# SyncE in written order in the q/k stage: weight tiles asked for a tile ahead, four forget pages per step between them

## The chip, the cores and the metric

The kernel runs on one core of a Trainium2 chip. A core has TensorE (PE, matrix products), VectorE (DVE), ScalarE (ACT), GpSimd (POOL) and SyncE (SP), which only issues transfers; each of them works through a queue of its own in order, and they wait for each other by semaphores. The metric is the device time of one run of the whole kernel in microseconds, the median of several runs.

## The reference

One inference step of a decoder of two layers over 1024 prompt tokens, 16 meta tokens and 64 sample tokens. The change sits in the first layer's mixer, and touches what prepares the second layer's cache:

```python
def mlstm_mixer(xn, C0, n0, m0, lead, w_in, b_ig, b_fg, mh_g, w_out):
    p = xn @ w_in
    q = heads(p[..., :HK], DK_A) * DK_A ** -0.5
    k = heads(p[..., HK:2 * HK], DK_A)
    v = heads(p[..., 2 * HK:2 * HK + HV], DV_A)
    ...
    li = softcap(gi.astype(f32) + b_ig.astype(f32)).transpose(0, 2, 1)
    lf = jax.nn.log_sigmoid(softcap(gf.astype(f32) + b_fg.astype(f32))).transpose(0, 2, 1)
    h, state = mlstm_sequence(q, k, v, li, lf, state0, lead)
    ...
    out = (h.reshape(B, T, HV).astype(xn.dtype) * jax.nn.sigmoid(og)) @ w_out

def attend_sample(q, k, v, lf):
    ...
    lp = cache_logf[page_table].reshape(Bd, n_pages * PAGE_SIZE, H_B)
    c = jnp.cumsum(jnp.concatenate([lp.astype(f32), lf], axis=1), axis=1)
```

`cache_logf[page_table]` gathers, for 8 sequences, 4 pages each of log-forget values: 32 pages, whose numbers stand in a table in memory.

## The kernel before

`phase_a` is the first mixer. First `values_a` computes the values, the gates and the first pieces of what follows. Then comes the q/k stage, 126.7 to 239.7 us on TensorE: the function `qk_out` makes q and k in 8 weight tiles of 128 output channels (m = 0 to 7), each against three token groups of 336, 384 and 384 columns (`TG`). So there are 24 steps; step x works on tile x // 3 and group x % 3. Each product in f32 is built from three matmuls of halves: the input is kept as xh and xl, and a weight tile is split into whi (a cast on ScalarE) and wlo (a subtraction on VectorE, raw minus whi). A step gathers its 24 matmuls (L193 to L195) in one of two PSUM buffers (`mmA`), ScalarE evacuates it into one of three buffers `stg` (L918), and GpSimd sends it to memory (L919). Step x therefore can't begin before step x - 2 has been evacuated.

The weights are loaded by `load_w`: a buffer `wraw` (there are two), a transfer of 512 KB asked for by SyncE (L256), the cast (L259) and the subtraction (L260) into one of three pairs of buffers. Below, "w_in m" is the weight tile m of the q/k stage, and "w_out m" is piece m of the output projection's weight, which is loaded, split and sent to memory (`wo_keep`, L875) for later use; the first three pieces and w_in 0 (`self.q0`) are done in `values_a`, by `wo_fetch` (transfer, L854) and `wo_split` (L271, L272).

Between the steps other work is written, by generators that are advanced at certain steps:

- `rec_prep`, at steps 1, 4 and 9: nine transposes each of the input gates (li) and the forget gates (lf) into buffers `rps`, of which there are two, by groups of three (L1098), each group copied by ScalarE (L1100); then scans and sums of these rows on VectorE (L1106 to L1132), with three exponentials on ScalarE (L1124, L1127, L1134); at step 9 their transposes back (L1140 to L1145).
- `cache_loads`: the page table into SBUF, then for each page a read of its number from SBUF into a register of SyncE (L1008, TENSOR_LOAD with two small instructions) and the transfer of the page at that number (L1010, FUSED_REGOPS, MOVE and the request), four pages per advance, at steps 0 to 7.
- `cache_prep`, at step 14: transposes the pages, sums them up and writes them out (eight requests of GpSimd, L1027).

The order of each engine's queue is set by a scheduler from the dependences, except for engines named in `manual_schedule`, which keep the written order. In this stage only TensorE is named there. For the others the scheduler chooses: it has set the page table and its 32 reads before 48 us, far ahead of their place in the text, and the 32 page requests into one block.

Of the kernel before, what the change touches and what calls it, by code (L numbers as in the profile page):

```python
# [17 lines left out]
P = 128  # L18
# [604 lines left out]
def _add(cls):  # L623
    def deco(f):
        setattr(cls, f.__name__, f)
        return f

    return deco
# [250 lines left out]
@_add(Net)  # L879
def phase_a(self, vt):  # L880
    nc, I, O = self.nc, self.I, self.O
    w_in = I["w_in_a"][0]
    qkD = self.dram.tile([8, P, T], F32, name="qkD")
    ogD = self.dram.tile([8, P, T], F32, name="ogD")
    v = lambda i: vt[:, i * HA * (DV + 1) : (i + 1) * HA * (DV + 1)].rearrange("p (h d) -> p h d", h=HA)
    with ExitStack() as c3:
        kp = c3.enter_context(self.pool("kA"))
        tm = kp.tile([P, NT, 104], F32, name="tmA")
        den = kp.tile([P, NT, HA], F32, name="den")
        ssq = kp.tile([P, NT, HA], F32, name="ssqA")  # L890
        self.C = [kp.tile([P, 4, DV + 1], F32, name=f"C{a}") for a in range(3)]
        gates = kp.tile([P, NT, 16], F32, name="gates")
        self.fin = (tm, den, ssq)
        for i in range(NT):
            nc.gpsimd.memset(v(i)[:, :, DV : DV + 1], 1.0)
        nc.gpsimd.memset(gates, 0.0)
        nc.gpsimd.memset(tm[:, 0, :], 0.0)
        nc.gpsimd.memset(den, 1.0)
        nc.gpsimd.memset(ssq, 1.0)
        st = c3.enter_context(self.pool("stA", bufs=3))  # L900
        self.woD, self.held = [], []
        self.values_a(v, kp, gates, w_in, c3)
        pp = c3.enter_context(self.pool("ppA", bufs=2, space=PSUM))

        def wo_out():
            m = len(self.woD)
            self.wo_keep(*self.load_w([I["w_out_a"][0][:, m * P : (m + 1) * P]]))

        def qk_out():

            for m in range(8):
                wh, wl = self.load_w([w_in[:, m * P : (m + 1) * P]]) if m else self.q0
                for t, (t0, t1) in enumerate(TG):
                    n = t1 - t0
                    ps = pp.tile([P, 512], F32, name=self.uid("mmA"), tag="mmA")
                    self.fm_cols(ps[:, :n], wh, wl, self.XG[t])
                    s = st.tile([P, GL], F32, name=self.uid("stg"), tag="stg")
                    nc.scalar.activation(s[:, :n], ps[:, :n], AF.Copy, scale=DK ** -0.5 if m < 4 else 1.0)  # L918
                    nc.gpsimd.dma_start(qkD[m, :, t0:t1], s[:, :n])  # L919
                    yield  # L920

        with self.pool("rowsA") as rp, self.pool("rowsAp", bufs=2, space=PSUM) as rpp, \
                self.pool("cp") as cp, self.tc.manual_schedule(engines={mybir.EngineType.PE}):
            pages = self.cache_loads(cp)
            prep = self.rec_prep(kp, gates, rp, rpp)
            next(prep)
            for x, _ in enumerate(qk_out()):
                if x in (1, 4, 9):
                    next(prep, None)
                next(pages, None)  # L930
                if x == 14:
                    self.cache_prep(*self.cache, rpp, "r")
                if x % 3 == 0 and 5 < x < 21:
                    wo_out()

        def gates_out():

            get = lambda m, later=None: self.load_w([w_in[:, (16 + m) * P : (17 + m) * P]], later=later)
            ws = [get(0)]
            later = []  # L940
            for m in range(8):
                wh, wl = ws[m]
                for t, (t0, t1) in enumerate(TG):
                    n = t1 - t0
                    ps = pp.tile([P, 512], F32, name=self.uid("mmA"), tag="mmA")
                    xh, xl = self.XG[t]
                    if t == 1 and m < 7:
                        ws.append(get(m + 1, later if m else None))
                    for k in range(KT):
                        if k == 6 and later:  # L950
                            later.pop()()
                        self.mm3(ps[:, :n], wh[:, k, :], wl[:, k, :], xh[:, k, :], xl[:, k, :], k == 0, k == KT - 1)
                        if k == KT - 1:
                            s = st.tile([P, GL], F32, name=self.uid("stg"), tag="stg")
                            nc.scalar.activation(s[:, :n], ps[:, :n], AF.Sigmoid)
                            nc.gpsimd.dma_start(ogD[m, :, t0:t1], s[:, :n])
                        yield

        left = {t: list(range(HA)) for t in range(3)}
        left[-1] = [None]  # L960

        def heads(pp, tag, op=None, some=None):

            ready, used = [], []
            todo = [(t, h) for t in (0, 1, 2) for h in left[t]][:some]

            def ahead():
                if todo:
                    t, h = todo.pop(0)
                    og = op(self.uid("ogc")) if callable(op) else op.pop(0)  # L970
                    nc.gpsimd.dma_start(og[:, : TG[t][1] - TG[t][0]], ogD[h, :, TG[t][0] : TG[t][1]])
                    ready.append(og)

            def gate(t):
                if not left[t]:
                    return False
                while todo and (len(ready) < 3 if callable(op) else op):
                    ahead()
                if t < 0:
                    return False  # L980
                og = ready.pop(0)
                self.gate_head(t, left[t].pop(0), v, og, pp, tag)
                if not callable(op):

                    used.append(og)
                    if len(used) > 1:
                        op.append(used.pop(0))
                return True
            return gate

        self.recurrence(kp, self.rec, v, qkD, gates_out(),
                        lambda places: heads(pp, "mmA", places, 10))
    return heads
# [2046 lines left out]
```

## Time and profile before

| | |
|---|---|
| time, median of 3 runs | 2832.24 us (2831.84 to 2833.01) |
| profiled execution | 2829.72 us, its span 2828.0 us, granted clock 0.994 |
| q/k stage | 126.7 to 239.7 us, TensorE busy for 105.73 of 113.00 us, clock 0.95 |
| before it, 0 to 126.7 us | TensorE busy for 115.77 us |
| after it, 239.7 to 2828 us | TensorE busy for 2540.44 of 2588.30 us |

In the time lines a row gives the start and the duration in us, the engine ("SPq" is a request by SyncE), the line, the operation, the destination and the sources by the names of the program, the shape, how many instructions were gathered in the row, and in square brackets how long the engine stood idle before it and what ended that. A row of the windows view gives a stretch, its length, the busy time of TensorE, its weight loads, VectorE, ScalarE and GpSimd, and then the granted clock of TensorE, the share of the transfer engines and GB/s. The matmuls overlap, so a matmul of 0.34 us is followed by the next after 0.17 us.

### The profile page before, as it was taken

The page shows a single profiled execution, that of the slowest core. Times are in us where ns is not written, and L with a number is a line of the kernel's source. Part 1 is how long each engine was busy: PE and PEld are TensorE (multiplying, and loading weights), DVE is VectorE, ACT ScalarE, POOL GpSimd, SP SyncE. Part 2 cuts the span into 40 slices and gives each one's busy share as a digit, 9 for nine tenths or more (in the row PEclk, how much of TensorE's full clock was granted, in tenths as well). Part 3 has the DMA queues.
Part 4 walks back from the last instruction along what each step waited for, and adds up shares of the span by engine and source line. Part 5 has one row for each costly group of instructions (what it writes and reads, how often), then busy time and mean ns, then how long its engine had stood idle before and what let it go on. Part 6 is the DMA issues. An engine that isn't in the chain of part 4 may idle for free. (4 is left out here: it accounts for less than half of the span.)

```text
span 2828.0 us, 60538 instructions
## 1 busy us (share of the span) xinstructions
PE 2761.9 (98%) x23543; PEld 2650.3 (94%) x23543; DVE 1800.4 (64%) x4025; ACT 1177.3 (42%) x2299; POOL 836.0 (30%) x1313
## 2 busy tenths in 40 slices
PE   8999999999999999999999999999999999999998
PEld 8989889999999999999999888677999999999998
DVE  4632566888887765563455444777388888766556
ACT  5422453432322334443444445777343223323345
POOL 3122233132232332124453202544313223323111
PEclk9999999999999999999999999999999999999999
DMA  6666547245554375545444676442524555527556
GB/s 196 171 196 162 144 125 255 90 143 165 176 167 148 112 243 174 195 145 171 139 172 132 237 279 226 154 143 86 157 83 128 175 176 164 161 90 239 178 191 215
DMA packets 439001, 474.03 MB, mean 168 GB/s; under 512 B 41422, under 2 KB 365258, under 8 KB 437690
## 3 DMA queue, kind: packets, MB, share of 16 engines
q1 hardware_dynamic: 387522, 320.78, 36.8%
q0 software_dynamic: 43808, 143.17, 15.3%
q10 hardware_dynamic: 7384, 6.22, 0.7%
q8 instruction: 185, 3.03, 0.5%
q14 instruction: 102, 0.84, 0.1%
HBM read 322.84 MB, written 147.21 MB: 166 GB/s over the span
## 5 line engine op out<-in xcount | busy, mean ns | idle before, releaser
L1611 PE MATMUL m<-xh,slot 128*128 128x276 f32 x2752 | 541.3, 290 | 1.8 <-ACT fs L1640 1.8
L1611 PEld LDWEIGHTS m<-xh,slot 128*128 128x128 f32 x2752 | 440.4, 188 | 3.6 <-ACT fs L1640 2.2
L1611 PE MATMUL m<-xl,slot 128*128 128x276 f32 x1376 | 397.4, 289 | 0.0
L1611 PEld LDWEIGHTS m<-xl,slot 128*128 128x128 f32 x1376 | 259.1, 188 | 0.0
L193 PE MATMUL tmps<-slot,xh 128*128 128x256 f32 (+2 forms) x864 | 243.1, 281 | 0.0
L195 PE MATMUL tmps<-slot,xl 128*128 128x256 f32 (+2 forms) x864 | 240.6, 278 | 0.0
L194 PE MATMUL tmps<-slot,xh 128*128 128x256 f32 (+2 forms) x864 | 240.5, 278 | 0.0
L272 DVE TENSOR_TENSOR slot<-slot,slot 128x1024 fp32r<-128x1024 f32 x124 | 162.9, 1314 | 60.7 <-ACT slot L271 59.2
L271 ACT CAST slot<-slot 128x1024 fp32r<-128x1024 f32 x124 | 129.6, 1046 | 141.2 <-PE m L1611 111.7
L194 PEld LDWEIGHTS tmps<-slot,xh 128*128 128x128 f32 (+1 forms) x864 | 159.2, 184 | 0.1
L195 PEld LDWEIGHTS tmps<-slot,xl 128*128 128x128 f32 (+1 forms) x864 | 158.6, 184 | 0.0
L193 PEld LDWEIGHTS tmps<-slot,xh 128*128 128x128 f32 (+1 forms) x864 | 158.4, 183 | 0.2
L193 PE MATMUL mmA<-xh,whi 128*128 128x384 f32 (+1 forms) x384 | 135.1, 352 | 0.0
L194 PE MATMUL mmA<-xl,whi 128*128 128x384 f32 (+1 forms) x384 | 127.9, 333 | 0.0
L195 PE MATMUL mmA<-xh,wlo 128*128 128x384 f32 (+1 forms) x384 | 127.7, 333 | 0.0
L272 DVE TENSOR_TENSOR slot<-vA,slot 128x1024 fp32r<-128x1024 f32 (+1 forms) x59 | 82.2, 1396 | 32.6 <-ACT slot L271 31.5
L272 DVE TENSOR_TENSOR slot<-Ht,slot 128x1024 fp32r<-128x1024 f32 (+1 forms) x59 | 81.4, 1382 | 32.3 <-ACT slot L271 31.1
L271 ACT CAST slot<-Ht 128x1024 fp32r<-128x1024 f32 (+1 forms) x59 | 61.0, 1037 | 96.8 <-PE m L1611 92.9
L271 ACT CAST slot<-vA 128x1024 fp32r<-128x1024 f32 (+1 forms) x59 | 60.8, 1035 | 95.5 <-PE m L1611 90.5
L1715 DVE TENSOR_TENSOR ws<-ws 128x128 f32<-128x128 f32 x264 | 93.8, 355 | 8.9
L2862 ACT ACTIVATE s<-s,nb 128x272 f32<-128x272 f32 (+7 forms) x126 | 98.9, 786 | 0.0
L2897 ACT COPY th<-tp 128x768 f32<-128x768 f32 (+1 forms) x80 | 73.6, 920 | 53.7 <-PE tp L2889 30.5
(805 smaller groups left out, 8668.8 us busy)
## 6 DMA issues: line engine op xcount, KB each, us to landing
ws<-in_w_down SPq DMA_DIRECT2D x176, 128.0 KB, 2.8
sD<-ws SPq DMA_DIRECT2D x176, 128.0 KB, 2.3
slot<-sD SPq DMA_DIRECT2D x40, 512.0 KB, 4.2
slot<-in_w_gate_up SPq DMA_DIRECT2D x36, 512.0 KB, 3.9
kp<-in_cache_k SPq DMA_DIRECT2D x32, 512.0 KB, 6.7
vp<-in_cache_v SPq DMA_DIRECT2D x32, 512.0 KB, 5.1
vA<-in_w_gate_up SPq DMA_DIRECT2D x26, 512.0 KB, 4.4
Ht<-in_w_gate_up SPq DMA_DIRECT2D x26, 512.0 KB, 3.9
```

The lines of the kernel that those rows point to most:

```text
L193: mm(ps, sh, mh, start=first, stop=False)
L194: mm(ps, sh, ml, start=False, stop=False)
L195: mm(ps, sl, mh, start=False, stop=last)
L271: self.nc.scalar.copy(hi, src)
L272: self.nc.vector.tensor_tensor(out=lo, in0=src, in1=hi.bitcast(F32), op=ALU.subtract)
L1611: nc.tensor.matmul(u.ps[h, b], w[p][:, k], x[q][:, k], start=first and k == i == 0, stop=k == 3 and i == 2, skip_group_check=True)
L1715: tt(out=o, in0=a, in1=b, op=ALU.subtract)
L2862: nc.scalar.activation(ss[z, u], ss[z, u], AF.Exp, bias=nb[:, z : z + 1], accum_out=sm[:, u, z : z + 1])
L2897: nc.scalar.copy(th.rearrange("p x z (u h q) -> p h (x z u) q", h=2, q=64)[:, :, :n], pt[:, :, :n])
```

## The change

SyncE keeps the written order in the q/k stage as well. The weights of this stage are no longer loaded by `load_w` at their tile, but in two halves: `wo_fetch` asks for w_in m + 1 at the first group of tile m, and for w_out m + 2 at the second group of tiles 1 to 5; `wo_split` casts and subtracts after the second and the third group's evacuation is written. The page table, the page reads and the page requests now stand between them in the written order, four pages per step from step 1 to step 8, and `cache_prep` comes at step 13. Line numbers behind the edit rise by one or two.

```diff
         def qk_out():
 
             for m in range(8):
-                wh, wl = self.load_w([w_in[:, m * P : (m + 1) * P]]) if m else self.q0
+                wh, wl = self.q0
                 for t, (t0, t1) in enumerate(TG):
+                    if t == 0 and m < 7:
+                        self.wo_fetch(w_in[:, (m + 1) * P : (m + 2) * P])
+                    elif t == 1 and 0 < m < 6:
+                        self.wo_fetch(m + 2)
                     n = t1 - t0
...
                     nc.gpsimd.dma_start(qkD[m, :, t0:t1], s[:, :n])
+                    if self.held and t:
+                        self.wo_split()
                     yield
 
         with self.pool("rowsA") as rp, self.pool("rowsAp", bufs=2, space=PSUM) as rpp, \
-                self.pool("cp") as cp, self.tc.manual_schedule(engines={mybir.EngineType.PE}):
+                self.pool("cp") as cp, self.tc.manual_schedule(engines={E.PE, E.SP}):
...
-                next(pages, None)
-                if x == 14:
+                if x:
+                    next(pages, None)
+                if x == 13:
                     self.cache_prep(*self.cache, rpp, "r")
-                if x % 3 == 0 and 5 < x < 21:
-                    wo_out()
```

`wo_out`, the function that loaded a piece of w_out by `load_w`, is removed. `wo_split` gives the halves of a w_in tile to the next tile's steps by `self.q0`, and those of a w_out piece to `wo_keep`. `cache_loads`, `cache_prep` and `rec_prep` are unchanged.

The order on SyncE at the head of the q/k stage, before. `wraw_108`, `wraw_120` and `wraw_132` are w_in 1, 2 and 3, `wraw_125` is w_out 3, and `cp0` receives the pages; the marks leave out pages.

```order
L256 DMA wraw_108_2097<-in_w_in_a 128x8x128
L256 DMA wraw_120_2355<-in_w_in_a 128x8x128
L256 DMA wraw_125_2429<-in_w_out_a 128x8x128
L1010 ISA
L1010 DMA cp0_1904<-in_cache_logf 128x16
...
L256 DMA wraw_132_2534<-in_w_in_a 128x8x128
L256 DMA wraw_140_2594<-in_w_out_a 128x8x128
L256 DMA wraw_147_2659<-in_w_in_a 128x8x128
```

All 32 pages stand in one block between w_out 3 and w_in 3, and the reads of the table are not here. The same engine and place now; `wraw_99`, `wraw_111` and `wraw_126` are w_in 1, 2 and 3, `wraw_114` and `wraw_129` are w_out 3 and 4, and `ptab` is the table.

```order
L854 DMA wraw_99_1874<-in_w_in_a 128x8x128
L1003 DMA ptab_70<-in_page_table 1x32
L1010 TENSOR_LOAD ptab_70
L1010 ISA x2
L1012 ISA
L1012 DMA cp0_1953<-in_cache_logf 128x16
...
L854 DMA wraw_111_2063<-in_w_in_a 128x8x128
...
L854 DMA wraw_114_2133<-in_w_out_a 128x8x128
...
L854 DMA wraw_126_2330<-in_w_in_a 128x8x128
...
L854 DMA wraw_129_2400<-in_w_out_a 128x8x128
```

The table and every read of it have come into the stage; 8 pages stand ahead of w_in 2, 4 ahead of w_out 3, 8 ahead of w_in 3, 4 ahead of w_out 4 and the last 8 behind it.

On ScalarE around steps 2 to 8, before: `whi` from `wraw_125` is the cast of w_out 3, that from `wraw_132` of w_in 3, `stg_107` to `stg_119` are the evacuations of steps 2, 3, 4 and 5.

```order
L259 CAST whi_126_2430<-wraw_125_2429 128x1024
L918 ACTIVATE stg_107_2054<-mmA_106_2029 128x384
L918 ACTIVATE stg_112_2128<-mmA_111_2103 128x336
L259 CAST whi_133_2535<-wraw_132_2534 128x1024
L918 ACTIVATE stg_114_2196<-mmA_113_2171 128x384
L1100 COPY lf_1871<-rps_115_2199 8x336
L1100 COPY lf_1871<-rps_116_2204 8x384
L1100 COPY lf_1871<-rps_117_2209 8x384
L1127 ACTIVATE stk_2231<-mA_1873 8x1104
L259 CAST whi_141_2595<-wraw_140_2594 128x1024
L918 ACTIVATE stg_119_2312<-mmA_118_2287 128x384
```

The cast of w_in 3 stands ahead of step 4's evacuation and of the copies of the forget rows. The same engine and place now; `stg_110`, `stg_113`, `stg_116`, `stg_123` and `stg_128` are the evacuations of steps 2 to 6, and the copies of `lf` from `rps_120` and `rps_121` are left out.

```order
L271 CAST whi_117_2163<-wraw_111_2063 128x1024
L919 ACTIVATE stg_110_2020<-mmA_109_1995 128x384
L271 CAST whi_124_2283<-wraw_114_2133 128x1024
L919 ACTIVATE stg_113_2090<-mmA_112_2065 128x336
L919 ACTIVATE stg_116_2160<-mmA_115_2135 128x384
L1102 COPY lf_1871<-rps_119_2167 8x336
...
L271 CAST whi_132_2430<-wraw_126_2330 128x1024
L1129 ACTIVATE stk_2199<-mA_1873 8x1104
L919 ACTIVATE stg_123_2280<-mmA_122_2255 128x384
L271 CAST whi_136_2502<-wraw_129_2400 128x1024
L1126 ACTIVATE wA_1869<-wA_1869 8x1104
L1136 ACTIVATE stk_2199<-bA_1872 8x1104
L919 ACTIVATE stg_128_2357<-mmA_127_2332 128x336
```

The casts of w_in 2 and w_out 3 now stand ahead of step 2's and step 3's evacuations, the cast of w_in 3 has moved behind the copies of `lf`, and two casts stand ahead of the evacuations of steps 5 and 6.

More of the change, by code (lines that the diff above doesn't have):

```diff
@@ L881, in phase_a @@
     nc, I, O = self.nc, self.I, self.O
+    E = mybir.EngineType
     w_in = I["w_in_a"][0]
@@ L903, in phase_a @@
         pp = c3.enter_context(self.pool("ppA", bufs=2, space=PSUM))
-        def wo_out():
-            m = len(self.woD)
-            self.wo_keep(*self.load_w([I["w_out_a"][0][:, m * P : (m + 1) * P]]))
         def qk_out():
             for m in range(8):
-                wh, wl = self.load_w([w_in[:, m * P : (m + 1) * P]]) if m else self.q0
+                wh, wl = self.q0
                 for t, (t0, t1) in enumerate(TG):
+                    if t == 0 and m < 7:
+                        self.wo_fetch(w_in[:, (m + 1) * P : (m + 2) * P])
+                    elif t == 1 and 0 < m < 6:
+                        self.wo_fetch(m + 2)
                     n = t1 - t0
```

## Prediction

> **What bounds the kernel now.** I read the page first, then the list of TensorE's waits, then the time lines of TensorE, ScalarE, VectorE and SyncE over the q/k stage, from 127 to 240 us. The page:
> ```profile
> span 2828.0 us, 60538 instructions
> PE 2761.9 (98%) x23543; PEld 2650.3 (94%) x23543; DVE 1800.4 (64%) x4025; ACT 1177.3 (42%) x2299; POOL 836.0 (30%) x1313
> ```
> TensorE is busy for 98% of the span, and the change alters none of its work; what can move are TensorE's waits in this stage and the speed at which it is clocked. Its largest wait there, in the list of waits (sum, count, mean, us), and its time line around it (start, duration):
> ```profile
> PE rps L1098 <- ACT lf L1100: 6.8, 1, 6.8
> ...
> 140.11 0.32 PE L193 MATMUL mmA<-xh,whi 128*128 128x336 f32 x1
> ...
> 143.80 0.34 PE L193 MATMUL mmA<-xh,whi 128*128 128x384 f32 x1
> ...
> 147.96 0.78 PE L1098 MATMUL rps<-ident,lf_tm 80*8 80x80 f32 x6
> 155.55 0.80 PE L1098 MATMUL rps<-ident,lf_tm 128*8 128x128 f32 x3 [6.80 <-ACT lf L1100]
> 156.00 0.67 PE L193 MATMUL mmA<-xh,whi 128*128 128x384 f32 x1
> ...
> 158.39 0.48 PE L194 MATMUL mmA<-xl,whi 128*128 128x384 f32 x1
> 158.70 0.34 PE L195 MATMUL mmA<-xh,wlo 128*128 128x384 f32 x1
> ```
> Step 3 begins at 140.11, step 4 at 143.80 and ends at 147.96: a step of 336 columns takes 3.69 us, one of 384 takes 4.16. Then six transposes of forget gates run, the last three find no free PSUM buffer for 6.80 us, and step 5, begun at 156.00, runs slow until 158.6 (0.48 to 0.67 us a matmul instead of 0.34). ScalarE at that place:
> ```profile
> 144.05 0.45 ACT L918 ACTIVATE stg<-mmA 128x336 f32<-128x336 f32 x1 [2.42 <-issue]
> 153.75 1.04 ACT L259 CAST whi<-wraw 128x1024 fp32r<-128x1024 f32 x1 [9.25 <-DMA wraw<-in_w_in_a]
> 154.70 0.48 ACT L918 ACTIVATE stg<-mmA 128x384 f32<-128x384 f32 x1
> 155.08 0.78 ACT L1100 COPY lf<-rps 8x336 f32<-8x336 f32 x2
> ```
> The cast of the weight tile (w_in 3) waits 9.25 us for its transfer, and behind it stand step 4's evacuation and the copies of the forget rows (L1100), which would free the buffer. SyncE says why the tile is late:
> ```profile
> 122.86 2.64 SPq L256 DMA_DIRECT2D wraw<-in_w_in_a  x2
> ...
> 130.71 0.37 SPq L256 DMA_DIRECT2D wraw<-in_w_out_a  x1
> 131.34 18.28 SPq L1010 DMA_DIRECT2D cp<-in_cache_logf  x32
> 149.74 0.39 SPq L256 DMA_DIRECT2D wraw<-in_w_in_a  x1
> ```
> The 32 forget pages stand in one block, 18.28 us long, ahead of w_in 3, asked at 149.74. The granted clock (the third number from the end) in stretches of 10 us:
> ```profile
> 150.00:160.00 10.00, 4.45 (x19) 4.29 (x20) 5.18 (x11) 2.58 (x5) 1.18 (x2) 0.66 0.67 179
> ...
> 180.00:190.00 10.00, 10.00 (x50) 9.92 (x50) 1.51 (x3) 1.54 (x2) 0.55 (x1) 0.83 0.71 207
> ```
> At 0.66 over 4.45 busy us the slow stretch costs 4.45 x 0.34 = 1.5 us. So the place costs 6.80 + 1.5 = 8.3 us, and that is all the change can win. The second dip (10 x 0.17 = 1.7 us) follows small transposes (L1140 to L1145) that both kernels have, and I leave it in both.
>
> **The change part by part.**
>
> *The page loop.* SyncE now reads a table entry into a register and asks for its page in one go, 32 times within the stage. Before, the 32 reads (L1008) were over by 48 us. Both halves, as min/median/max ns, the one wait for the table, and the median time from asking a weight tile to its landing:
> ```profile
> L1008 SPq TENSOR_LOAD <-ptab x32: 262/275/1086, 12.7 to 47.3; - x32
> L1008 SPq FUSED_REGOPS  x32: 147/147/181, 13.2 to 47.6; - x32
> L1008 SPq SEQ_ASSERT  x32: 18/18/33, 13.4 to 47.8; - x32
> ...
> L1010 SPq FUSED_REGOPS  x32: 37/37/48, 131.1 to 149.2; - x32
> L1010 SPq MOVE cp<-in_cache_logf x32: 29/29/38, 131.3 to 149.2; - x32
> L1010 SPq DMA_DIRECT2D cp<-in_cache_logf x32: 332/333/1267, 131.3 to 149.3; - x32
> ...
> SPq L1008 <- DMA ptab<-in_page_table: 4.2, 1, 4.2
> ...
> wraw<-in_w_in_a SPq DMA_DIRECT2D x22, 512.0 KB, 4.2
> ```
> One page before took 18.28 / 32 = 0.57 us, of which 37 + 29 + 333 ns are instructions, so 0.17 is three gaps of 0.06. The read adds 0.275 + 0.147 + 0.018 + three such gaps = 0.61. **A page: 0.57 + 0.61 = 1.18 us.** Bounds: 1.07 (with every gap of the read left out, 0.57 + 0.44 = 1.01, and shortest read) up to 0.57 + 0.61 + 0.81 = 1.99, if each read were like the slowest, 1.086. I take the median, as the forget pages run at 157 to 207 GB/s or so and the slow reads fell in the first 48 us, where a stretch reached 392 GB/s:
> ```profile
> 25.00:30.00 5.00, 4.13 (x37) 3.97 (x36) 4.36 (x10) 4.05 (x10) 0.86 (x1) 1.00 1.03 392
> ...
> 140.00:150.00 10.00, 8.74 (x56) 8.29 (x54) 1.38 (x2) 1.89 (x3) 2.17 (x4) 1.00 0.53 157
> ```
> A sentence apart: the Trainium skill, "Runtime: NRT & Kernel Launch", section "Instruction fetch mechanics", gives about 200 ns for a register read; the estimate by it would be 1.10 us a page and about 1.7 us less than my sum, and the 262 ns minimum here does not agree.
>
> *Requests in written order.* Now the order is w_in 1, the table, 8 pages, w_in 2, 4 pages, w_out 3, 8 pages, w_in 3, 4 pages, w_out 4, 8 pages, then weights alone. w_in 1 is asked at 122.86 as before, so the table at 123.3 and, with the same 4.2 us of wait, the first read at 127.8. Each weight costs 0.4 to ask and 4.2 to land:
> w_in 2 asked 127.8 + 8 x 1.18 = 137.2, lands 141.4; w_out 3 asked 142.4, lands 146.6; w_in 3 asked 152.2, lands 156.4; w_out 4 asked 157.3, lands 161.5. All pages are asked by 167. The matmuls need w_in 2 at step 6 and w_in 3 at step 9, so these are early enough for TensorE itself; what bites is that ScalarE takes its queue in order, and the casts of these four now stand among evacuations.
>
> *ScalarE's queue, step by step* (cast 1.05, evacuation 0.45 to 0.48):
> Step 4 needs step 2's buffer. Cast of w_in 2 ends 142.5, evacuation of step 2 143.0, step 4 due 143.80: covered, with 0.8 to spare.
> Step 5: the cast of w_out 3 ends 147.6, then evacuations of steps 3 and 4 until 148.55 and the first forget copy until 148.95. TensorE comes to its third transposes at 147.96 + 0.78 = 148.7: a wait of 0.25 instead of 6.80. Step 5 starts at 148.95 + 0.5 = 149.45 (before: 156.00).
> Step 7 needs step 5's buffer, due 149.45 + 4.16 + 3.69 = 157.3. Ahead of that evacuation stand the cast of w_in 3 (to 157.45) and the exponential of mA (1.13, to 158.6); it ends at 159.1. **New wait 1.9 us**.
> Step 8 needs step 6's buffer, due 159.2 + 4.16 = 163.4. Ahead stand the cast of w_out 4 (161.5 to 162.6) and the exponentials of wA and bA; their rows before, and the work on VectorE that feeds them:
> ```profile
> 165.42 1.21 DVE L1122 TENSOR_TENSOR wA<-eA,mA 8x1024 f32<-8x1024 f32 x1
> ...
> 166.82 1.20 DVE L1132 TENSOR_TENSOR bA<-stk,eA 8x1024 f32<-8x1024 f32 x1
> ...
> 161.75 1.13 ACT L1127 ACTIVATE stk<-mA 8x1104 f32<-8x1104 f32 x1 [4.90 <-DVE mA L1110]
> ...
> 166.66 1.13 ACT L1124 ACTIVATE wA<-wA 8x1104 f32<-8x1104 f32 x1 [0.79 <-DVE wA L1122]
> ...
> 170.66 1.12 ACT L1134 ACTIVATE stk<-bA 8x1104 f32<-8x1104 f32 x1
> ```
> 162.6 + 1.13 + 1.12 + 0.48 = 165.3. **New wait 2.0 us**. This one has a floor: bA was ready 12.94 us after the first forget copy (166.82 + 1.20 - 155.08), so at 148.55 + 12.94 = 161.5 at best; then 1.12 and 0.48 give 163.1, against 157.3 + 4.16 = 161.5, so 1.65 remain however fast SyncE is.
> Later weights stand behind no pages: w_in 4 is asked near 167 and cast by 173, step 12 comes after 180.
>
> *Parts at nothing.* The reads leave the first 48 us; TensorE's wait there that is nearest to them, 1.99 us (row below), was for a cast, and I credit nothing; bounds nil to -2.0. Preparing the forget rows a step earlier has the same four transposes and eight requests on GpSimd (count, then busy us and mean ns):
> ```profile
> L1027 POOL DMA_DIRECT2D csE<-cp x8 | 4.3, 544 | 1.7 <-DVE clast L1025 1.3 <-issue 0.4
> ```
> GpSimd's other work there is one request a step, so evacuated tiles leave at most 4.3 us later; the three evacuation buffers, about 12 us of steps, hide that, and without them it would cost up to 4.3. Splits of weights move but keep their number.
>
> *The clock.* Does a wait of 2 us halve it? The nearest row is an early wait:
> ```profile
> 32.36 0.52 PE L193 MATMUL tmps<-whi,xh 128*80 128x272 f32 x1 [1.99 <-ACT whi L271]
> ...
> 30.00:35.00 5.00, 3.01 (x13) 2.44 (x12) 3.99 (x10) 4.02 (x12) 0.85 (x1) 0.74 0.74 199
> ```
> After 1.99 us without work the clock was 0.74 over these 5 us, so yes, once. The dip of 180 to 190 cost 1.7 in all, which I take as the price. With two waits of this size, bounds are none and 3.4 us; I take one, 1.7.
>
> **The sum.** Before 8.3; after 0.25 + 1.9 + 2.0 + 1.7 = 5.85, so -2.4 us. On the profiled execution (2829.72 us, span 2828.0) that gives 2827.3; this execution was 2.52 below the median of 2832.24, and I forecast the median: **2829.8 us**. 24 pages stand ahead of w_out 4, so 0.1 us more a page costs 2.4 us; the gain is gone at 1.18 + 2.4 / 24 = 1.28 us a page.
>
> A measurement of this kernel tells about 0.2% from no change, 5.7 us: faster is below 2826.6, slower above 2837.9.
>
> **The rivals.**
> B, *the two new waits don't touch the clock*: -2.4 - 1.7 = -4.1, 2828.1 us. For it: an overlap of a 2 us wait with busy time on both sides; against it, the row at 32.36. The Trainium skill, "TensorE: Matmul & The Clock Gate", section "What's actually happening", has the clock halved only after an idle window of about 3.4 us; by that rule B holds, while the 1.99 us wait of this trace, followed by 0.74, does not agree with it.
> C, *faster beyond doubt*: the reads run near 1.07 a page, w_out 4 lands 2.6 us sooner, step 7's wait goes and step 8's falls to its floor; with no dip 0.25 + 1.65 = 1.9 remain, so -6.4, 2825.8 us. For it: 262 to 275 ns are both minimum and median of the reads. Against it: it needs the clock to hold too.
> D, *slower: SyncE's page loop sets the pace.* Every weight now waits behind reads that SyncE can't run ahead of. If reads stretch as they did up to 1086 ns, or gaps do, each cast comes late, ScalarE holds evacuations behind it and TensorE waits at steps 4, 5, 7 and 8. From 1.18 + 8.1 / 24 = 1.52 us a page it is slower than can be missed; at 1.6 it gives -2.4 + 0.42 x 24 = +7.7, 2839.9 us, and at 1.99 some +17. For it: the maximum is four times the median, and pages have traffic beside them; against it: the median lies by the minimum.
> That SyncE's order stays as it was is excluded: the rows of the order shown with the change have the weights among the pages.
>
> **How the numbers follow.** My forecast has 0.38, B 0.20, C 0.17, D 0.25. Within 0.2% lie the forecast and B: 0.58. The range reaches to C's -6.4 with a little under it, 2825.5, and to D at 1.6 us a page, 2840; left out are slower pages than that.
>
> **What would show it.** In the profile after: the wait of the third transposes under 0.5 us; pages as triplets of a read, a register step and a request, 1.1 to 1.3 us apart from 127.8 on; casts of w_in 3 and w_out 4 released by their transfers at about 156.4 and 161.5; waits of 1 to 2.5 us ahead of steps 7 and 8 by ScalarE's evacuations; the clock under 1 once after one of them. I am wrong if pages come 1.5 us apart, if a wait over 4 us stands at step 4 or 5 (then w_in 2 or w_out 3 was later than worked out), or if the time moves outside this stage.

## The result, and the profile after

Over 20 runs each, the changed kernel takes 2834.07 us (median) and the kernel before 2831.02. The ratio on record is 1.0018 (95% interval 1.0012 to 1.0024); it isn't the quotient of these two medians, which is 1.0011. So the changed kernel is slower by some 3 to 5 us; the forecast was 2.4 us faster. The profiled execution has a span of 2829.8 us, 1.8 above that of before, so it shows less of the loss than the medians. The two lists of waits answer each other; this is TensorE's list after, from 120 to 250 us:

```profile
PE mmA L193 <- ACT stg L919: 9.8, 1, 9.8
PE rps L1100 <- ACT lf L1102: 0.7, 1, 0.7
```

The wait of 6.8 us for the forget rows has shrunk to 0.7, as meant. A single wait of 9.8 us has come in its place, for an evacuation. The first gate transposes and the first evacuation behind the stage bound it, in the time lines of TensorE and ScalarE, first before, then after:

```profile
134.57 0.78 PE L1098 MATMUL rps<-ident,gates 80*8 80x80 f32 x6
244.73 0.45 ACT L955 ACTIVATE stg<-mmA 128x336 f32<-128x336 f32 x1
```
```profile
133.21 0.78 PE L1100 MATMUL rps<-ident,gates 80*8 80x80 f32 x6
248.48 0.45 ACT L957 ACTIVATE stg<-mmA 128x336 f32<-128x336 f32 x1
```

110.16 us became 115.27, so the stage lost 5.1. Waits account for 9.8 + 0.7 - 6.8 = 3.7 of it, most of the rest is the clock, below. Around the stage this execution got some back. It began the stage 1.4 us earlier, since it had no half-speed stretch at 32 us (a second trace of the changed kernel has it again, at 33.1 us). Behind the stage it got back 1.9 us, 1.5 of them where before ran at half speed from 257.7 us on and this one didn't.

SyncE after (start, duration, count):

```profile
127.97 8.72 SPq L1012 DMA_DIRECT2D cp<-in_cache_logf  x8
136.79 0.39 SPq L854 DMA_DIRECT2D wraw<-in_w_in_a  x1
137.97 3.70 SPq L1012 DMA_DIRECT2D cp<-in_cache_logf  x4
141.77 0.39 SPq L854 DMA_DIRECT2D wraw<-in_w_out_a  x1
142.96 9.56 SPq L1012 DMA_DIRECT2D cp<-in_cache_logf  x8
152.62 0.39 SPq L854 DMA_DIRECT2D wraw<-in_w_in_a  x1
154.13 3.71 SPq L1012 DMA_DIRECT2D cp<-in_cache_logf  x4
159.67 0.39 SPq L854 DMA_DIRECT2D wraw<-in_w_out_a  x1
160.85 9.90 SPq L1012 DMA_DIRECT2D cp<-in_cache_logf  x8
170.85 0.47 SPq L854 DMA_DIRECT2D wraw<-in_w_in_a  x1
```

The weights are asked for almost at the forecast times: w_in 2 at 136.8 (137.2), w_out 3 at 141.8 (142.4), w_in 3 at 152.6 (152.2). Then ScalarE and TensorE:

```profile
163.53 1.04 ACT L271 CAST whi<-wraw 128x1024 fp32r<-128x1024 f32 x1 [14.40 <-DMA wraw<-in_w_in_a]
164.60 1.12 ACT L1129 ACTIVATE stk<-mA 8x1104 f32<-8x1104 f32 x1
165.74 0.49 ACT L919 ACTIVATE stg<-mmA 128x384 f32<-128x384 f32 x1
```
```profile
166.29 0.69 PE L193 MATMUL mmA<-xh,whi 128*128 128x384 f32 x1 [9.82 <-ACT stg L919]
```

The cast of w_in 3 begins 10.9 us after its transfer was asked for, not 4.2; behind it stand the exponential and step 5's evacuation, and step 7 waits for that. So it is the path that the prediction gave for step 7, with a far longer landing. The transfers issued from 148 to 160 us (KB, median us to landing), and the windows view around them (transfer share and GB/s at the end of a row):

```profile
woD<-wlo POOLq DMA_DIRECT2D x1, 512.0 KB, 10.8
wraw<-in_w_in_a SPq DMA_DIRECT2D x1, 512.0 KB, 10.8
...
out_s_m<-mA POOLq DMA_DIRECT2D x1, 0.2 KB, 9.9
out_p_m<-mA POOLq DMA_DIRECT2D x1, 0.0 KB, 9.5
```
```profile
150.00:152.00 2.00, 2.00 (x14) 2.00 (x13) 2.00 (x2) 0.00 (x0) 0.64 (x1) 1.00 1.02 368
152.00:154.00 2.00, 2.00 (x14) 2.00 (x13) 2.00 (x2) 0.00 (x0) 0.00 (x0) 1.00 0.38 81
154.00:156.00 2.00, 2.00 (x15) 2.00 (x14) 2.00 (x2) 0.00 (x0) 0.52 (x1) 1.00 1.57 57
156.00:158.00 2.00, 0.47 (x4) 0.19 (x2) 0.40 (x1) 0.00 (x0) 0.00 (x0) 1.00 0.77 28
158.00:160.00 2.00, 0.00 (x0) 0.00 (x0) 0.00 (x0) 0.00 (x0) 0.00 (x0) 1.00 0.40 17
```

The transfer engines are occupied, yet move 17 to 81 GB/s: single packets of w_in 3 take up to 5.9 us, against 27 ns for the median packet of its size. Two very small writes are in flight, both outputs of the layer asked by GpSimd: out_s_m, 64 numbers of 4 bytes each for scattered places (at 150.05), and out_p_m, 8 numbers (at 154.28). Before, out_s_m was asked at 157.74, and from 160 to 164 us nothing else was on the way:

```profile
160.00:162.00 2.00, 2.00 (x14) 2.00 (x13) 2.00 (x2) 0.24 (x1) 0.00 (x0) 1.00 0.00 0
162.00:164.00 2.00, 2.00 (x15) 2.00 (x14) 2.00 (x2) 1.98 (x3) 0.52 (x1) 1.00 0.01 0
```

### The profile page after: what moved, and what is told of

It reads as the page before. It is cut to its first block, busy times and chain, and to the rows that moved or that the text cites. A ratio compares the mean times of both kernels' runs of the same rounds, so it can differ in the third digit from the quotient of the medians.

```text
span 2829.8 us, 60544 instructions
## 1 busy us (share of the span) xinstructions
PE 2758.6 (97%) x23543; PEld 2646.6 (94%) x23543; DVE 1797.7 (64%) x4025; ACT 1176.8 (42%) x2299; POOL 835.5 (30%) x1313
```

## The experiments

Each ratio is to the kernel before on the same chip, with its 95% interval. A stage length is measured as above, from the first gate transposes to the first evacuation behind the stage (110.16 us before, 115.27 in the changed kernel).

**The changed kernel once more** (no edit).

> The changed kernel once more, unaltered. In its first trace w_in 3 was asked at 152.62 us and its cast began at 163.53, 10.9 us later instead of the 4.2 forecast, and step 7 waited 9.82 us. Theory S (the two small output writes of mA, asked at 150 and 154 us, hold up the transfers beside them) and theory P (the forget pages beside it do): the late landing is there again, 8 us or more, step 7 waits 7 to 10 us, ratio to before 1.001 to 1.003. Theory C (chance of that execution): it lands in 4 to 5 us, step 7 waits about 2, and the time is no more than before's.

1.0021 (1.0012 to 1.0030). w_in 3 was asked at 153.30 and cast at 163.92, 10.6 us later, and step 7 waited 9.22 us. The late landing is no chance (C falls).

**The small writes later, first try.**

```diff
-            nc.gpsimd.dma_start(O["p_m"]..., m[:, T - 1 : T])        # in rec_prep, step 4
-            nc.gpsimd.dma_start(O["s_m"]..., m[:, NQ - 1 : NS : NQ])
...
             nc.vector.tensor_copy(wcS, ps[:, 1])                      # end of rec_prep, step 9
+            nc.gpsimd.dma_start(O["p_m"]..., m[:, T - 1 : T])
+            nc.gpsimd.dma_start(O["s_m"]..., m[:, NQ - 1 : NS : NQ])
```

> The changed kernel with the writes of out_p_m and out_s_m moved from step 4 to step 9. Theory S: w_in 3 lands within 5 us of being asked, step 7 waits 1 to 3 us, some 6 us less than the changed kernel: ratio to before 0.998 to 1.000. Theories P and C: as the unaltered changed kernel of the same call, within 0.1%.

1.0019 (1.0009 to 1.0028), and w_in 3 landed as late (153.98 to 164.94). But this is no verdict on S: the trace has out_s_m asked at 151.85, where it was. GpSimd's order is the scheduler's, and the edit moved nothing.

**The reads of the page table first, in one block.**

```diff
         self.woD, self.held = [], []
+        nc.sync.dma_start(self.ptab, ...)
+        self.pages = [nc.sync.value_load(self.ptab[0:1, j : j + 1], ...) for j in range(NPG * NB)]
         self.values_a(v, kp, gates, w_in, c3)
```

> The changed kernel with the page table and its 32 reads ahead of the value stage, so that a page in the q/k stage costs 0.57 us instead of 1.2. w_in 3 is then asked about 12 us sooner, near 139 us, ahead of the small writes. Theory S: it lands in 4 to 5 us, no wait of step 7 above 1 us, ratio to before 0.997 to 0.999. Theory P: pages twice as dense beside w_in 2 and w_in 3 make these land in 8 us or more, and step 5 or 7 waits 2 us or more.

1.0031 (1.0020 to 1.0042), for another reason: SyncE did the 32 reads ahead of the inputs, and TensorE waited 17.13 us for xin at the start. In the stage itself no wait was over 1.6 us, and it was 102.95 us long. The run doesn't tell S from P, since everything in it lies 12 us later.

**The pages in steps 9 to 16.**

```diff
-                if x:
+                if x > 8:
                     next(pages, None)
-                if x == 13:
+                if x == 21:
```

> The changed kernel with the four pages per step in steps 9 to 16 instead of 1 to 8, and their preparation at step 21. No page stands ahead of w_in 2, 3, 4 or w_out 3, 4. Theories S and P: all of them land before ScalarE comes to their casts, steps 5, 7 and 8 together wait under 1.5 us, ratio to before 0.996 to 0.998. If pages beside weights slow them (P), w_in 5 or 6 now lands in 8 us or more; by S it lands in 4 to 5.

1.0000 (0.9991 to 1.0009). The waits of steps 4 to 8 are gone, and the stage's last part came 6.6 us earlier than before's. Then TensorE waited behind it:

```profile
PE n0p L1316 <- DMA n<-in_state_n: 9.5, 1, 9.5
```

SyncE asked for the recurrent state at 236 us instead of 216, behind the later page preparation. The gain of the stage was given back to that wait, which the expectation had missed. w_in 5 and 6, with pages around them, were cast 5.3 and 6.5 us after they were asked, so pages beside a weight don't make it land as late as theory P has it (8 us or more).

**Both small writes asked by SyncE at step 21; and out_s_m alone.**

```diff
-            nc.gpsimd.dma_start(O["p_m"]..., m[:, T - 1 : T])
-            nc.gpsimd.dma_start(O["s_m"]..., m[:, NQ - 1 : NS : NQ])
+            self.small = lambda: (nc.sync.dma_start(O["p_m"]..., ...), nc.sync.dma_start(O["s_m"]..., ...))
...
+                if x == 21:
+                    self.small()
```

> The changed kernel with the writes of out_p_m and out_s_m asked by SyncE at step 21, behind the last weight of the stage; in the earlier attempt (e2_small_late) GpSimd's order is the scheduler's, and it had left them where they were (151.85 and 156.08 us). Theory S (these two writes hold up the transfers beside them): w_in 3 is cast within 5 us of being asked, step 7 waits 1 to 3 us instead of 9.2 to 9.8, ratio to before 0.998 to 1.000. Theory W (what holds w_in 3 up is the write of the weight piece woD, 512 KB on GpSimd's queue just ahead of it, or the pages): w_in 3 is cast 8 us or more after it was asked, ratio 1.001 to 1.003 as before.

> As e5_small_step21, but only out_s_m (64 numbers) is moved; out_p_m (8 numbers), asked 4 us later, stays on GpSimd at step 4. If out_s_m is what holds the transfers up: w_in 3 cast within 5 us, as in e5_small_step21. If it is out_p_m: w_in 3 is cast 8 us or more after it was asked. If neither (theory W), the same 8 us or more.

On the cause both say S, and out_s_m: w_in 3 was cast 4.7 us after it was asked (152.39 to 157.10) and 4.4 with out_s_m alone moved (155.10 to 159.52), with the write of the weight piece and the pages where they were: neither of these does it alone (W and P fall). Step 7 waited 3.02 and 3.46 us instead of 9.2 to 9.8. But both are slower still, 1.0045 (1.0032 to 1.0058; and to 1.0059). The first, with both writes moved, has out_s_m asked at 202.53, and the stall is there:

```profile
202.53 0.32 SPq L1116 DMA_DIRECT2D out_s_m<-mA  x1
```
```profile
206.00:208.00 2.00, 2.00 (x15) 2.00 (x14) 1.23 (x1) 0.45 (x2) 1.59 (x3) 1.00 3.00 182
208.00:210.00 2.00, 2.00 (x14) 2.00 (x13) 0.00 (x0) 0.45 (x1) 0.00 (x0) 1.00 1.16 54
210.00:212.00 2.00, 2.00 (x14) 2.00 (x13) 0.00 (x0) 0.00 (x0) 0.00 (x0) 1.00 0.38 32
```
```profile
214.50 0.54 POOL L920 DMA_DIRECT2D qkD<-stg  x1 [6.91 <-DMA csE<-cp]
221.19 1.04 ACT L271 CAST whi<-wraw 128x1024 fp32r<-128x1024 f32 x1 [11.82 <-DMA woD<-whi]
```
```profile
178.13 0.58 PE L1144 MATMUL tps<-ident,stk 104*128 104x104 f32 x4 [3.46 <-DVE tmA L1145]
222.68 0.65 PE L193 MATMUL mmA<-xh,whi 128*128 128x336 f32 x1 [5.53 <-ACT stg L919]
```

What it holds up there are the eight writes of the prepared pages (csE, 256 KB each): they took 11.3 us to land instead of 4.9 in the changed kernel. GpSimd waits 6.91 us for one of them and asks for the write of a weight piece only at 215.15; the next cast needs that piece's buffer, and TensorE waits 5.53 us. And without the first stall a wait of 3.46 us has appeared at step 9, which the changed kernel doesn't have.

**Pages in steps 4 to 11, small writes at step 21** (`if x > 3: next(pages, None)`, and the edit above).

> The changed kernel with the pages in steps 4 to 11 instead of 1 to 8, their preparation still at step 13, and both small writes asked by SyncE at step 21. No page stands ahead of w_in 2 and w_out 3, 8 ahead of w_in 3, 12 ahead of w_out 4, and the page buffer is free early enough for the recurrent state that is loaded into it, which was missed in e4_pages_late (TensorE waited 9.5 us for n behind the stage). Theory S: waits of steps 4 to 8 together under 2 us, the stage some 6 to 8 us shorter than before's, ratio 0.997 to 0.999. Theory W: w_in 3 or w_out 4 takes 8 us or more after a write of woD, and the ratio is 0.999 to 1.001.

1.0012 (1.0003 to 1.0021): neither theory's picture. w_in 3 was cast 5.3 us after it was asked, the third transposes (ahead of step 5) waited 2.86 us, and the write at step 21 cost 6.44 us of wait, as above. Two effects are mixed in this run.

**SyncE left to the scheduler** (`engines={E.PE}`), the fetch ahead alone.

> The changed kernel with SyncE left to the scheduler (only TensorE in written order), so that the change is the fetch ahead alone. By its order the 32 page reads are early again, and w_in 1, w_in 2 and w_out 3 stand ahead of 20 pages, then w_in 3, 9 pages and w_out 4. The 20 pages take 11.4 us at 0.57 each, so w_in 3 is asked about 143 us, some 6 us before before's 149.74, and cast before the small writes start: no wait of step 4 to 8 above 1.5 us, ratio 0.997 to 0.999 by all theories; slower than 1.000 would mean that the order of SyncE matters in a way that none of them has.

0.9995 (0.9987 to 1.0004). No slower than before, possibly faster; the third transposes waited 2.88 us, more than expected. The stage is 107.62 us long. Against the changed kernel's 1.0018, what loses lies in SyncE's queue: its written order, or the reads that this order puts into the stage. The two are told apart by the last two runs.

**out_s_m turned by TensorE, written as 8 rows of 32 bytes.** In the changed kernel, in the one left to the scheduler, and in the kernel before. The edit also moves the write to step 9, so it is asked at 185 us instead of 150 in the changed kernel:

```diff
-            nc.gpsimd.dma_start(O["s_m"][0].rearrange("b h -> h b"), m[:, NQ - 1 : NS : NQ])
...
+            nc.tensor.transpose(ps[:NB, :HA], m[:, NQ - 1 : NS : NQ], self.ident[:HA, :HA])
+            nc.vector.tensor_copy(smT, ps[:NB, :HA])
+            nc.gpsimd.dma_start(O["s_m"][0], smT)
```

> The changed kernel with out_s_m turned first: TensorE transposes its 8 x 8 numbers at step 9, and GpSimd writes 8 rows of 32 bytes instead of 64 single numbers of 4 bytes scattered by the transfer. Theory S4 (the single 4-byte numbers are what blocks the transfers): no stretch in which 512-byte or 4096-byte packets take microseconds, w_in 3 cast within 5 us, waits at steps 7 and 8 of about 3.0 and 1.8 and before the transposes of step 9 of about 3.5 as with the write at step 21, but no wait of 5.5 at step 22; so the stage 5 to 7 us shorter than in e5_small_step21, ratio to before 1.000 to 1.002. Theory S8 (any small write of this tensor does it): a stall of 7 us now lies near step 9 to 11 and some cast or evacuation there is late.

> The kernel of e8_sync_scheduled (fetch ahead, SyncE left to the scheduler) with the same turned write of out_s_m. By S4 nothing of that kernel's waits changes much, since its stall lay beside weights that had slack: ratio to before 0.998 to 1.000, within 0.1% of e8_sync_scheduled; by S8 slower than that by 0.1% or more.

> The kernel before with the turned write of out_s_m alone. Its stall of 157.7 to 164.6 us lay in a gap in which nothing else was asked for, so by S4 nothing is gained: ratio 0.999 to 1.001, the 6.8 us wait of the forget transposes unchanged. A gain over 0.15% would mean that the write costs before something that its trace does not show.

1.0016 (1.0007 to 1.0025), 0.9997 (0.9988 to 1.0006) and 1.0001 (0.9992 to 1.0010). In the first, no data packet from 150 to 206 us takes over 0.9 us, and w_in 3 was cast 4.2 us after it was asked. So the late landing comes with the write at 150 us. Whether its scattered form is what stalls (S4) isn't shown: the turned write was also 35 us later, and no run has the scattered one at that place. Yet the time hardly moved; the stage is 114.63 us long. TensorE's waits there, and the windows with its clock:

```profile
PE mmA L193 <- ACT stg L919: 3.5, 3, 2.6
PE tps L1141 <- DVE tmA L1142: 3.2, 1, 3.2
PE rps L1100 <- ACT lf L1102: 0.3, 1, 0.3
```
```profile
160.00:170.00 10.00, 8.70 (x39) 8.38 (x40) 5.23 (x9) 4.93 (x7) 4.05 (x7) 0.83 0.57 175
170.00:180.00 10.00, 6.76 (x44) 6.35 (x42) 3.12 (x4) 2.93 (x4) 2.15 (x4) 0.94 0.81 210
180.00:190.00 10.00, 10.00 (x38) 9.72 (x38) 2.17 (x5) 1.04 (x1) 0.52 (x1) 0.55 0.89 269
```

The waits, 3.5 + 3.2 + 0.3 = 7.0, are as much as before's 6.8, so they don't explain a stage 4.5 us longer than before's. Most of that is the clock: 8.70 x 0.17 + 6.76 x 0.06 + 10 x 0.45 = 6.4 us lost, against 3.2 before. The half-speed stretches begin at 161.7 us, behind the wait at step 7 (2.65 us), and at 178.8, near the end of the wait at step 9 (3.24 us). The new wait, at step 9, in the time lines of SyncE, ScalarE and VectorE:

```profile
169.43 0.39 SPq L854 DMA_DIRECT2D wraw<-in_w_in_a  x1
```
```profile
175.00 1.05 ACT L271 CAST whi<-wraw 128x1024 fp32r<-128x1024 f32 x1 [2.61 <-DMA wraw<-in_w_in_a]
```
```profile
176.08 1.23 DVE L272 TENSOR_TENSOR wlo<-wraw,whi 128x1024 fp32r<-128x1024 f32 x1 [9.43 <-ACT whi L271]
177.73 1.22 DVE L272 TENSOR_TENSOR wlo<-wraw,whi 128x1024 fp32r<-128x1024 f32 x1 [0.42 <-ACT whi L271]
178.87 0.75 DVE L1142 COPY tmA<-tps 80x104 f32<-80x104 f32 x2
```

w_in 4, asked at 169.4 behind all 32 pages, is cast at 175.0, and VectorE's queue has its subtraction and the next one ahead of the copies that free the transposes' buffers.

**The reads out of the stage, SyncE's written order kept.** The table and its reads are written ahead of the stage, outside the written order, so the scheduler puts them among the first loads, as before; once with the turned write, once with nothing else changed.

```diff
         pp = c3.enter_context(self.pool("ppA", bufs=2, space=PSUM))
+        nc.sync.dma_start(self.ptab, ...)
+        self.pages = [nc.sync.value_load(self.ptab[0:1, j : j + 1], ...) for j in range(NPG * NB)]
...
-            v = nc.sync.value_load(self.ptab[0:1, j : j + 1], ...)   # in cache_loads
-            self.pages.append(v)
+            v = self.pages[j]
```

> The kernel of e9_s_m_rows with the page table and its 32 reads written ahead of the q/k stage, outside the written order, where the scheduler puts them among the first loads as before did (in e3_reads_early they stood in one block ahead of everything and TensorE waited 17 us at the start, so that run couldn't tell). SyncE keeps the written order in the stage with pages at 0.57 us. Theory R (the reads inside the stage make the weights late): w_in 3 is asked near 142 us instead of 154, w_in 4 before 162 instead of 169, the waits of 2.65 at step 7 and 3.24 at step 9 shrink to under 1 together, ratio to before 0.997 to 0.9995. Theory O (it is the written order): those waits stay above 4 us together and the ratio at 1.001 or more.

> The same without the turned write, so the changed kernel with nothing but the reads taken out. Out_s_m's write then blocks the transfers from about 153 to 160 us. Theory R: w_in 3 has landed by then and what is blocked (w_out 4, w_in 4) has slack, as in e8_sync_scheduled: waits of steps 5 to 9 together under 4 us, ratio 0.998 to 1.000, within 0.1% of e12_reads_out_rows. Theory O: ratio 1.001 or more.

0.9985 (0.9976 to 0.9994) and 0.9982 (0.9973 to 0.9991). Theory R. In the second, SyncE and TensorE's waits:

```profile
135.16 4.05 SPq L1012 DMA_DIRECT2D cp<-in_cache_logf  x8
140.39 0.39 SPq L854 DMA_DIRECT2D wraw<-in_w_in_a  x1
...
151.35 0.39 SPq L854 DMA_DIRECT2D wraw<-in_w_in_a  x1
```
```profile
PE rps L1100 <- ACT li L1102: 1.9, 1, 1.9
PE mmA L193 <- ACT stg L922: 0.7, 2, 0.3
PE rps L1100 <- ACT lf L1102: 0.3, 1, 0.3
```

w_in 3 is asked at 140.4 instead of 152.6, w_in 4 at 151.4 instead of 170.9. The square of two by two:

| ratio to before | out_s_m scattered | out_s_m turned, at step 9 |
|---|---|---|
| reads in the stage | 1.0018 and 1.0021 | 1.0016 |
| reads out of the stage | 0.9982 | 0.9985 |

The reads are worth 0.0031 to 0.0039, some 9 to 11 us, where a single ratio is known to 0.0009. The stage lengths say the same: 115.27 and 114.63 us with the reads inside, 105.38 and 106.07 outside. The scattered write is worth nothing that shows in either row. With the reads inside, the weights are late with and without it. With the reads outside it held up nothing: from 152.6 to 160.9 us, while it was under way, no packet took over 0.75 us. The kernel with the reads out and nothing else is faster than the kernel before and the changed one.

## Why the prediction was wrong, point by point

- **What bounds the place: right.** The wait of the third transposes was behind the cast of w_in 3, and went from 6.80 to 0.74 when the pages were split (0.25 forecast).
- **A page of 1.18 us: right.** 9.56 us for 8 is 1.20; 32 reads measured 263/270/881 ns. SyncE's requests came within 0.6 us of the forecast up to w_in 3.
- **"Each weight costs 0.4 to ask and 4.2 to land": the step that failed in the trace.** 4.2 is a median over transfers of the whole kernel. For w_in 3 it was 10.9, beside out_s_m; the wait at step 7 was 9.8 instead of 1.9. Waits of 9.8 + 0.7 in place of 4.15 and 0.7 more for the clock (below) turn -2.4 into +4.7, against the 5.1 by which the stage is longer. That the forget rows are ready 7 us sooner also moved out_s_m 7.7 us earlier, from a gap without traffic into w_in 3. I had followed the forget rows' chain on VectorE and ScalarE, but not the write that it releases on GpSimd.
- **"Later weights stand behind no pages": the step that failed in the sum.** Without the stall, steps 7 and 8 waited 2.65 and 0.32 us (turned write) or 3.02 and 1.80 (both writes at step 21); 1.9 and 2.0 were forecast, so that part is near. But w_in 4 and w_out 5 still stood behind the last 8 pages, and I compared w_in 4 only with step 12, which needs it. VectorE's queue has their subtractions ahead of step 9's copies: 3.24 us that the sum doesn't have. So the landing was not the only fault: with 4.2 us measured for it, the change still loses.
- **One half-speed stretch, 1.7 us: near in the changed kernel, but by luck.** From 150 to 190 us before lost 1.5 + 1.7 = 3.2. After, these windows give 3.71 x 0.43 + 10 x 0.08 + 10 x 0.17 = 4.1; the forecast was 3.4. The clock was in fact halved for 10.2 us from 161.3 on, but TensorE stood waiting for half of that. With the write turned, where two waits of 2.65 and 3.24 us came, it lost 6.4.

```profile
160.00:170.00 10.00, 3.71 (x12) 3.71 (x13) 5.36 (x9) 6.08 (x7) 2.17 (x4) 0.57 0.60 151
170.00:180.00 10.00, 10.00 (x57) 10.00 (x56) 1.63 (x3) 3.07 (x5) 2.20 (x4) 0.92 0.75 235
180.00:190.00 10.00, 9.80 (x53) 9.23 (x52) 2.84 (x7) 1.50 (x2) 1.61 (x3) 0.83 0.86 263
```

- **Rivals.** D named what decides, the reads that SyncE can't run ahead of, and the reads-out runs show it. Its price was wrong: it had the loss from 1.28 us a page and a loss beyond doubt from 1.52, while at the measured 1.2 the change already loses. Both limits were worked out from the sum above, with a landing of 4.2 and without step 9. B did not come to pass: with the write turned, the waits of 2.65 and 3.24 us each came with a half-speed stretch.

## What to carry to other kernels

When requests are put into written order, everything that the queue does in that place counts, scalar reads too: take them out first (here 0.61 of 1.18 us a page, 0.3% of the kernel), then interleave. For each late tile, look through the queues of all engines for what stands behind its cast and its subtraction, not only for the step that consumes it. When a chain moves earlier, follow what it releases as well, down to writes of 256 bytes.

## What the runs showed of the hardware

In six traces the transfers of all queues were held up for about 7 us while a write of 64 scattered 4-byte numbers was under way: from 153 to 161 us in the changed kernel, where GpSimd asks for it, and from 206 to 213 us with both small writes asked by SyncE at step 21. Single packets took up to 5.9 and 6.5 us there, and up to 6.9 us in all six. The write alone isn't enough. With the reads in one block, the pages in steps 9 to 16, SyncE left to the scheduler, and the reads out with nothing else, the same scattered write took 7.2 to 8.8 us beside 0.5 to 1.1 MB of other transfers, and no packet took over 0.75 us. In the six traces GpSimd had large writes under way at the same time (512 KB of a weight piece, or the eight of csE); in the four neither of these ran until the last 1.1 us. No run tests this alone. Written as 8 rows of 32 bytes it held up nothing, but later and beside no such write. Eight numbers of out_p_m, in one row of memory, left on GpSimd at step 4 when out_s_m was moved, held up nothing either. The Trainium skill, "DMA: Bandwidth & Descriptors", section "Issuing engines are not separate DMA queues", has transfers asked by different engines run on the same 16 DMA engines; this agrees, since beside a write of GpSimd's those of SyncE were held up. Why they stall is not settled by these runs.

Whether a wait of 2 to 3 us halves TensorE's clock depends on more than its length. 1.99 us in the trace of before and 2.88 in the one with SyncE left to the scheduler were followed by 3.4 us at half speed; 1.94 (reads out), 2.86 (pages in steps 4 to 11) and 3.0 (the changed kernel, at 32 us) were not. The half-speed stretches of these traces last 3.4, 6.8 or 10.2 us, apart from the one at the kernel's end. The Trainium skill, "TensorE: Matmul & The Clock Gate", section "What's actually happening", gives a free-running window of 3413 ns; the lengths agree with it. So do the starts: within one trace they lie whole multiples of 3.413 us apart (before: 32.39, 151.86, 182.58 and 257.67 us, so 35, 9 and 22 steps). Laid on that grid, the wait of 2.88 us falls whole into one step (148.45 to 151.86 us), at whose end the clock is halved; the wait of 2.86 us at the same place in the program is cut by the grid into 1.37 and 1.49, and nothing follows. The grid doesn't lie at the same place in every run (the first stretch begins at 32.39 us in before's trace, at 33.09 in the second of the changed kernel), which can explain part of the spread of 10 us among 20 runs of one kernel; the limit within a step isn't worked out here.
